# An encoder layer with long convolutions: weight loads issued from ScalarE, and one row copied instead of loaded

## The chip, the cores and the metric

The kernel runs on one core of one Trainium2 chip. Its time is the device time in microseconds (us), given as the median of 3 runs. A core has five engines, each with its own instruction stream: TensorE (PE) does matrix products, VectorE (DVE), ScalarE (ACT) and GpSimd (POOL) do elementwise work, and SyncE (SP) mainly starts transfers (DMAs) between the chip's memory and the on-chip buffer. In the profile, "PEld" is TensorE's loading of stationary operands, and a name with q behind it ("SPq", "ACTq") is that engine's sequencer: the part that waits and starts transfers.

## The reference

One layer of an encoder is computed in fp32 for two inputs with the same weights: group A, 1024 tokens ("prompt"), and group B, 512 tokens ("sample"), both 1024 features wide.

```python
mod = silu(c) @ ada_w + ada_b                       # six vectors: shift, scale, gate, twice
u = rmsnorm(x) * (1 + sc1) + sh1
z = u @ w_in                                        # 1024 -> 2304 (z_hy), 3 x 768 (q, k, v), 2048 (g)
zc = short_conv(z_hy);  x0, x1, v = split(zc)
y_hy = x0 * long_conv(x1 * v, k2, hyena_d)          # by FFT of twice the length
y_at = dilated_attention(q, k, v, rel_bias)         # 3 groups of 4 heads, dilation 1, 4, 16
g_hy, g_at = split(sigmoid(g))
h = x + gt1 * ((g_hy * (y_hy @ w_hy_br) + g_at * (y_at @ w_at_br)) @ w_out)
y = h + gt2 * (relu(rmsnorm(h) * (1 + sc2) + sh2) @ w_up)**2 @ w_down
```

The filter `k2` of the long convolution is itself computed, by a small network with sines, and is used through its spectrum. In a real FFT the values at frequency zero and at the highest frequency are real, and the kernel keeps the second in the place of the first one's imaginary part. That packed row is the row that the change is about.

## The kernel before, in words

**Layout.** Features lie on the 128 partitions and tokens along the free axis. Group A's tokens take two products of 512 columns, group B's take one.

**Products.** Every large product is done in three passes: each operand is split into a high part and the remainder, and `mm3` (its products are line 750) adds wh·xh, wh·xl and wl·xh over eight blocks of 128 features.

**Units.** The weights come as units, one 128 x 1024 tile (512 KB) for each block of 128 outputs. For each unit:
- `wdma` (line 456) loads the raw tile into a buffer `wr`; there are two of them. Four units have a second chunk, of `w_at`, in a buffer of the common pool.
- `wsplit` makes the two parts: ACT copies the tile to `wh` (line 389, CAST in the profile), and VectorE, or GpSimd in the stage qkvB, subtracts to get `wl` (line 390). When the subtraction has ended the raw buffer is free.
- the unit's body runs the 24 (group B) or 48 (group A) products and evacuates the result.

**The stream.** `stream` (line 471) walks through all units. At unit i it writes into the program, in this order: the load of unit i+2, the split of unit i+1, and the body of unit i. Between the products of the body, `pump` lets side work run: generators for the attention, the filter, the convolutions and the norms, paced by a clock that the program keeps from estimated costs. `finish` completes a side job that a later unit needs.

**Order.** ACT's instructions stand in the order in which the program writes them (it is fixed by hand for the whole kernel). The order on SP, VectorE, GpSimd and TensorE is chosen by a planner that keeps the dependences, but for the start, where TensorE's and VectorE's is fixed too. Nearly all transfers are started by SP: `dma` is SyncE's.

**Stages.** In the order of time: the start; the projections of group A (qkvA and zhyA); its gates (gateA); the projections of group B (qkvB, zhyB) and its gates (gateB); the merge of A and of B (mixA, mixB); the MLPs (ffA, ffB). The convolutions of A run as side work beside group A's projections and gates, those of B beside zhyB, gateB and what follows.

**The convolution** (`conv_gen`) runs three times for each group, once for each third of the 768 channels. `stage1` transforms blocks and stores them to the chip's memory. `middle` (line 934) loads them back in another order (line 894), loads the filter's spectrum in two tiles `ka` (line 939) and `kb` (line 940), each in halves of 64 partitions, and constant matrices (line 882), multiplies by a matrix (line 952), by the spectrum (lines 953 to 956), by a second matrix (line 963), and stores (line 969). Then the tiles are loaded in the last order (line 977), multiplied (line 989), and gated by `x0` (line 993). Up to several `middle` run at once.

In the first `middle` of each convolution the packed row needs care:

```python
if eg == 0:
    dma(ka[64:65, 0], S.spec[th][64:65, 0])
    V.memset(kb[0:1, 0], 0.0)
    V.memset(kb[64:65, 0], 0.0)
```

Row 64 of `ka` has been loaded from row 0 of the spectrum (the upper half of `ka` is a second copy of rows 0 to 63), and line 942 loads row 64 of the spectrum over it: 256 numbers. It can start when the load of that half of `ka` has landed. Row 64 of the spectrum is also what the load of `kb` has put in row 0 of `kb`, which line 943 then sets to zero.

Of the kernel before, what the change touches and what calls it, by code (L numbers as in the profile page):

```python
# [325 lines left out]
def _program(ctx, tc, d, outs):  # L326
# [9 lines left out]
    V, A, T, G_ = nc.vector, nc.scalar, nc.tensor, nc.gpsimd  # L336
    dma = nc.sync.dma_start
# [14 lines left out]
    def nm(s):  # L352
        cnt[0] += 1
        return f"{phase[0]}__{s}{cnt[0]}"

    def g(shape=(1024,), dt=F32):
        return gp.tile([128, *shape], dt, tag="g", name=nm("g"))
# [7 lines left out]
    def pss2():  # L365
        return pss().rearrange("p (a b) -> p a b", a=2)
# [6 lines left out]
    def copy(out, in_):  # L373
        rr[0] += 1
        if rr[0] % CPM:
            A.copy(out, in_)
        else:
            V.tensor_copy(out, in_)
# [70 lines left out]
            yield r[0], 0.0  # L449
        yield 0.0, max(end - clock[0], 0.0)  # L450

    def wdma(u):
        u.raw = []
        for i, (src, n) in enumerate(u.chunks):
            raw = g() if i else wp.tile([128, 1024], F32, tag="wraw", name=nm("wr"))
            dma(raw[:, :n], src)
            u.raw.append(raw)

    def wsplit(u):
# [11 lines left out]
    def stream(units, first=0):  # L471
        n = len(units)
        for i, (name, u) in enumerate(units):
            if i < first:
                continue
            phase[0] = name
            if u.before:
                u.before()
            if i + 2 < n:
                wdma(units[i + 2][1])  # L480
            if i + 1 < n:
                wsplit(units[i + 1][1])
            for c in u.body(u.w):
                pump(c, u.ratio)
            u.w = None
            if u.after:
                u.after()
# [22 lines left out]
    def spread_load():  # L510
        t = g((640,))
        dma(t, d["c_spread"])
        V.tensor_copy(spread, t[:, 0:512].rearrange("p (a b) -> p a b", a=4))
        return t[:, 512:640]
# [52 lines left out]
    def ada_load(qt):  # L567
        wts = []
        for k2 in range(4):
            wt = g((2, 512))  # L570
            w = dma(wt, d["ada1"][qt, k2].rearrange("p (a b) -> p a b", a=2))
            wts.append(wt)
        return wts, w.ins
# [306 lines left out]
    def cmat(src, eg):  # L880
        cm = wp.tile([128, 4, 128], F32, tag="cm", name=nm("cm"), bufs=4)
        dma(cm, src[eg])
        return cm

    def stage2_load(S, s1, eg):

        Q, nt = S.Q, S.nt
        nl = 64 // Q
        v = s1.rearrange("j p c -> (j p) c").rearrange("(q r l e) c -> r l q e c", q=Q, r=2, l=nl, e=nt)
        t = g((4, 256))  # L890
        for r in range(2):
            for l in range(nl):
                p0 = 64 * r + Q * l
                dma(t[p0:p0 + Q], v[r, l][:, 4 * eg:4 * eg + 4])
        return t


    def conv_gen(S, th):
# [35 lines left out]
        def middle(eg):  # L934
            sin = stage2_load(S, s1, eg)
            ka, kb = g((4, 256)), g((4, 256))
            es = slice(4 * eg, 4 * eg + 4)
            for hf in range(2):
                dma(ka[64 * hf:64 * hf + 64], S.spec[th][0:64, es])
                dma(kb[64 * hf:64 * hf + 64], S.spec[th][64:128, es])  # L940
            if eg == 0:
                dma(ka[64:65, 0], S.spec[th][64:65, 0])
                V.memset(kb[0:1, 0], 0.0)
                V.memset(kb[64:65, 0], 0.0)
            cm, cb_ = cmat(S.fw, eg), cmat(S.bw, eg)
            yield 0.0, LLD
            y, vv = g((4, 256)), g((4, 256))
            for ep in range(2):
                e2 = slice(2 * ep, 2 * ep + 2)
                ps = pss2()  # L950
                for ee in range(2):
                    T.matmul(ps[:, ee], cm[:, 2 * ep + ee], sin[:, 2 * ep + ee], start=True, stop=True)  # L952
                V.tensor_tensor(y[:, e2], ps, ka[:, e2], ALU.mult)
                V.scalar_tensor_tensor(vv[0:64, e2], ps[64:128], -1.0, kb[0:64, e2], ALU.mult, ALU.mult)
                V.tensor_tensor(vv[64:128, e2], ps[0:64], kb[64:128, e2], ALU.mult)
                G_.tensor_tensor(y[:, e2], y[:, e2], vv[:, e2], ALU.add)
                yield 0.9, LY if ep else 0.0
            del sin, ka, kb, vv
            so = g((4, 256))
            for ep in range(2):  # L960
                ps = pss2()
                for ee in range(2):
                    T.matmul(ps[:, ee], cb_[:, 2 * ep + ee], y[:, 2 * ep + ee], start=True, stop=True)
                copy(so[:, 2 * ep:2 * ep + 2], ps)
                yield 0.9, 0.0
            for r in range(2):
                for l in range(nl):
                    p0 = 64 * r + Q * l
                    dma(v2[r, l][:, 4 * eg:4 * eg + 4], so[p0:p0 + Q])

        yield from par([middle(eg) for eg in range(nt // 4)], WMID)
        yield 0.0, 3.0
        bt = []
# [661 lines left out]
    u0, u1 = units[0][1], units[1][1]  # L1635
    loads = [ada_load(0)]
    f1u = spread_load()
    wdma(u0)
    loads.append(ada_load(1))
    wdma(u1)  # L1640
    loads += [ada_load(2), ada_load(3)]
    last = loads[3][1]

# [39 lines left out]
def build(arrays):  # L1683
    nc = bacc.Bacc("TRN2", target_bir_lowering=False, num_devices=1)
    d = {n: nc.dram_tensor(n, a.shape, mybir.dt.from_np(a.dtype), kind="ExternalInput").ap()
         for n, a in arrays.items()}
    outs = [nc.dram_tensor(n, s, F32, kind="ExternalOutput").ap()
            for n, s in (("out_a", (8, 128, LA)), ("out_b", (8, 128, LB)))]
    with tile.TileContext(nc) as tc:
        with ExitStack() as ctx:  # L1690
            ctx.enter_context(tc.manual_schedule(engines={mybir.EngineType.Activation}))
            _program(ctx, tc, d, outs)
    return nc
# [10 lines left out]
```

## Time and profile before

| | |
|---|---|
| median of 3 runs | 2721.21 us (2716.90 to 2723.11) |
| the profiled execution | 2719.46 us |
| its span in the trace | 2717.7 us |
| granted clock of TensorE, mean | 0.976 of full speed |
| busy: PE / PEld / DVE / ACT / POOL | 2622.7 / 2123.4 / 1217.9 / 861.2 / 241.4 us |
| moved by transfers | 350.97 MB, 129 GB/s over the span |

The span goes from the first to the last event in the trace of one execution; the 1.8 us between it and that execution's own time lie around it. "Busy" counts the time in which an engine works on an instruction; waits, and the starting of transfers, are not counted. Engines work side by side, so their busy times do not add up to the span. A row of the timeline gives the start and the length in us, the engine, the line, the operation, output <- inputs, and in brackets how long the engine had waited before it and for whom. A row of the waits gives who waited at which line, for whom, and then the total in us, the number of waits and the longest.

### The profile page before, as it was taken

The numbers are of one execution on the slowest core, as the hardware profiler recorded it, in microseconds if no ns is written. First come the engines' busy times: TensorE is split into PE (matmuls) and PEld (weight loads), VectorE is DVE, ScalarE is ACT, GpSimd is POOL, SyncE is SP. The second block draws the span as 40 slices with busy tenths as digits, with TensorE's granted clock in tenths as the row PEclk, the third lists the DMA queues.
The fourth block names the chain that finished last, engine by engine and source line by source line (L and its number), as shares of the span: only waits on it lengthen the run. The fifth ranks groups of instructions, "written<-read, shape, count | busy, mean of one in ns | idle before, by whom it ended". The sixth has DMA issues, their size and how long they took to land.

```text
span 2717.7 us, 30781 instructions
## 1 busy us (share of the span) xinstructions
PE 2622.7 (97%) x12296; PEld 2123.4 (78%) x12296; DVE 1217.9 (45%) x1566; ACT 861.2 (32%) x1414; POOL 241.4 (9%) x162
## 2 busy tenths in 40 slices
PE   7999799999999999998999999999999999999999
PEld 4778687778788777777787887888888888888887
DVE  4454352443567633464334455333333333554544
ACT  3543312243243354443243243122112211232322
POOL 0101110100001243000012221000000000000000
PEclk8999898999999999999999999999999999999999
DMA  6355576615655432467663343111111111422322
GB/s 255 120 159 168 169 197 178 195 52 148 197 193 205 151 128 99 132 190 212 218 226 105 120 163 113 47 49 45 55 47 48 54 47 47 147 100 94 99 95 101
DMA packets 138113, 350.97 MB, mean 129 GB/s; under 512 B 19023, under 2 KB 50316, under 8 KB 137843
## 3 DMA queue, kind: packets, MB, share of 16 engines
q1 hardware_dynamic: 137682, 348.23, 39.3%
q8 instruction: 97, 1.59, 0.2%
q0 software_dynamic: 288, 0.79, 0.1%
q14 instruction: 46, 0.37, 0.0%
HBM read 280.68 MB, written 71.16 MB: 129 GB/s over the span
## 4 chain that ended last, share of the span: by engine, by line
PE 56%; DVE 2%; DMA 2%; ACT 1%; issue 1%; SPq 1%; POOL 0%; DVEq 0%; ACTq 0%; POOLq 0%
PE ffA__mm L750 26%; PE ffB__mm L750 13%; PE mixA__mm L750 6%; PE qkvB__mm L750 2%; PE gateB__mm L750 2%; PE zhyB__mm L750 2%; PE mixB__mm L750 2%; DMA convB__g<-convB__dr 1%; PE convB__s L989 1%; ACT attB__sc L1221 0%; DMA convB__g<-filtB__dr 0%; PE convB__s L952 0%; PE filtB__s L872 0%; DVE mixB__wl L390 0%; PE attB__s L1231 0%
## 5 line engine op out<-in xcount | busy, mean ns | idle before, releaser
L750 PE MATMUL ffA__mm<-ffA__g,ffA__wh 128*128 128x512 f32 x1024 | 274.1, 389 | 0.0
L750 PE MATMUL ffA__mm<-normA__g,ffA__wh 128*128 128x512 f32 x992 | 265.2, 389 | 0.0
L750 PEld LDWEIGHTS ffA__mm<-ffA__g,ffA__wh 128*128 128x128 f32 x1024 | 192.0, 188 | 40.5 <-issue 0.4
L750 PEld LDWEIGHTS ffA__mm<-normA__g,ffA__wh 128*128 128x128 f32 x992 | 186.2, 188 | 38.6
L1486 DVE SCALAR_TENSOR_TENSOR mixA__g<-ffA__mm,adam,mixA__g 128x1024 f32<-128x1024 f32 x64 | 82.1, 1283 | 190.1 <-PE ffA__mm L750 190.1
L750 PE MATMUL ffB__mm<-ffB__g,ffB__wh 128*128 128x512 f32 x512 | 157.7, 389 | 0.0
L750 PE MATMUL ffA__mm<-ffA__g,ffA__wl 128*128 128x512 f32 x512 | 157.7, 389 | 0.0
L750 PE MATMUL zhyA__mm<-init__g,zhyA__wh 128*128 128x512 f32 x512 | 150.3, 412 | 7.2 <-DVE zhyA__g L1012 5.6
L750 PE MATMUL ffA__mm<-normA__g,ffA__wl 128*128 128x512 f32 x496 | 152.8, 389 | 0.0
L750 PE MATMUL ffB__mm<-normB__g,ffB__wh 128*128 128x512 f32 x496 | 152.7, 389 | 0.0
L389 ACT CAST ffA__wh<-ffA__wr 128x1024 fp32r<-128x1024 f32 x63 | 66.0, 1048 | 256.7 <-PE ffA__mm L750 213.7
L1468 DVE SCALAR_TENSOR_TENSOR ffA__g<-ffA__mm,ffA__g 128x1024 f32<-128x1024 f32 x32 | 39.2, 1225 | 222.8 <-ACT ffA__g L1467 222.8
L750 PE MATMUL gateA__mm<-init__g,gateA__wh 128*128 128x512 f32 x480 | 132.4, 396 | 0.0
L750 PE MATMUL qkvA__mm<-init__g,qkvA__wh 128*128 128x512 f32 x416 | 120.5, 407 | 0.0
L750 PE MATMUL mixA__mm<-mixA__g,mixA__wh 128*128 128x512 f32 x424 | 116.0, 395 | 3.8 <-DVE mixA__g L390 3.3
L750 PEld LDWEIGHTS zhyA__mm<-init__g,zhyA__wh 128*128 128x128 f32 x512 | 95.5, 192 | 30.2 <-ACT zhyA__wh L389 7.9
L750 PEld LDWEIGHTS ffB__mm<-ffB__g,ffB__wh 128*128 128x128 f32 x512 | 96.0, 188 | 20.3 <-ACT ffB__g L389 0.2
L750 PEld LDWEIGHTS ffA__mm<-ffA__g,ffA__wl 128*128 128x128 f32 x512 | 96.1, 188 | 20.0
L1467 ACT ACTIVATE ffA__g<-ffA__mm 128x1024 f32<-128x1024 f32 x32 | 33.0, 1030 | 237.9 <-PE ffA__mm L750 237.9
L750 PEld LDWEIGHTS ffB__mm<-normB__g,ffB__wh 128*128 128x128 f32 x496 | 93.1, 188 | 19.3
L750 PEld LDWEIGHTS ffA__mm<-normA__g,ffA__wl 128*128 128x128 f32 x496 | 93.1, 188 | 19.3
L750 PEld LDWEIGHTS gateA__mm<-init__g,gateA__wh 128*128 128x128 f32 x480 | 90.4, 190 | 19.0 <-issue 0.6
(487 smaller groups left out, 5105.2 us busy)
## 6 DMA issues: line engine op xcount, KB each, us to landing
ada__g<-ada SPq DMA_DIRECT2D x32, 512.0 KB
ffA__wr<-w_up SPq DMA_DIRECT2D x32, 512.0 KB
ffA__wr<-w_dn SPq DMA_DIRECT2D x32, 512.0 KB
ffB__wr<-w_dn SPq DMA_DIRECT2D x32, 512.0 KB
ffB__wr<-w_up SPq DMA_DIRECT2D x30, 512.0 KB
filtA__dr<-filtA__g SPq DMA_DIRECT2D x24, 512.0 KB
convA__g<-filtA__dr SPq DMA_DIRECT2D x48, 256.0 KB
init__g<-ada SPq DMA_DIRECT2D x16, 512.0 KB
```

The source lines that it names most:

```text
L389: A.copy(hi, raw)
L750: T.matmul(ps[:, 512 * c:512 * c + 512], ww[:, sl], xx(k)[:, 512 * c:512 * c + 512], start=k == 0 and p == 0, stop=k == kt - 1 and p == 2)
L989: T.matmul(ps[:, :, 4 * j8:4 * j8 + 4], bt[j // 4][:, j % 4, 128 * cc:128 * cc + 128], ibm, start=True, stop=True)
L1467: A.activation(r, ps[:, :L], AF.Relu)
L1468: V.scalar_tensor_tensor(r, ps[:, :L], 0.0, r, ALU.max, ALU.mult)
L1486: V.scalar_tensor_tensor(S.h(m), ps[:, :L], mod(S, 5, m), S.h(m), ALU.mult, ALU.add)
```

## The change

The weight loads of `wdma` are started from ACT's queue (`A.dma_start`) and no longer from SP's. The first two units, which are loaded ahead of the stream, are still loaded from SP. All other transfers stay where they were. As ACT's order is that of the program, the load of unit i+2 stands on ACT right ahead of the cast of unit i+1 (or behind side work that was written before it).

The one-row load of line 942 is replaced by a copy on VectorE from row 0 of `kb`, ahead of the memset that sets that row to zero. It happens six times: once in each convolution of each group. `V` is VectorE and `A` is ScalarE.

```diff
-    def wdma(u):
+
+    def wdma(u, issue=A.dma_start):
         u.raw = []
         for i, (src, n) in enumerate(u.chunks):
             raw = g() if i else wp.tile([128, 1024], F32, tag="wraw", name=nm("wr"))
-            dma(raw[:, :n], src)
+            issue(raw[:, :n], src)
             u.raw.append(raw)
...
             if eg == 0:
-                dma(ka[64:65, 0], S.spec[th][64:65, 0])
+                V.tensor_copy(ka[64:65, 0], kb[0:1, 0])
                 V.memset(kb[0:1, 0], 0.0)
                 V.memset(kb[64:65, 0], 0.0)
...
-    wdma(u0)
+    wdma(u0, dma)
     loads.append(ada_load(1))
-    wdma(u1)
+    wdma(u1, dma)
```

## The prediction

> **What bounds the kernel now.** I read the page first, then the table of engine time in stretches of 50 us, then the waits, then the timelines around each stall of TensorE (PE).
>
> ```profile
> span 2717.7 us, 30781 instructions
> PE 2622.7 (97%) x12296; PEld 2123.4 (78%) x12296; DVE 1217.9 (45%) x1566; ACT 861.2 (32%) x1414; POOL 241.4 (9%) x162
> PEclk8999898999999999999999999999999999999999
> PE 56%; DVE 2%; DMA 2%; ACT 1%; issue 1%; SPq 1%; POOL 0%; DVEq 0%; ACTq 0%; POOLq 0%
> ```
>
> PE is busy for 2622.7 of 2717.7 us, so at most 95 us are idle. A change in who issues loads removes no product. It can only change those idle microseconds, and the stretches in which PE ran at a lower granted clock. In the next rows the columns are the stretch, its length, busy time of PE, PEld, DVE, ACT and POOL (with instruction counts), granted clock, DMA share and GB/s.
>
> ```profile
> 400.00:450.00 50.00, 46.19 (x222) 40.21 (x221) 15.45 (x23) 15.53 (x24) 2.58 (x2) 0.83 0.77 224
> 1200.00:1250.00 50.00, 42.07 (x198) 34.89 (x197) 24.36 (x33) 14.69 (x22) 5.17 (x4) 0.90 0.74 221
> 1250.00:1300.00 50.00, 44.30 (x203) 35.61 (x201) 24.25 (x32) 16.76 (x25) 5.18 (x4) 0.99 0.71 204
> 1300.00:1350.00 50.00, 47.88 (x221) 39.98 (x222) 17.40 (x21) 10.85 (x15) 6.14 (x4) 0.94 0.71 229
> 2450.00:2500.00 50.00, 50.00 (x222) 41.43 (x221) 24.22 (x28) 13.95 (x17) 0.00 (x0) 1.00 0.29 101
> ```
>
> The MLP (the last row stands for it) keeps PE full at full clock with DMA at 29%. The idle time lies in the long convolutions' stretches, where DMA is 71 to 77% busy and the clock falls. So the question is what the change does there, and whether it breaks the MLP.
>
> **The change, part 1: loads leave SP.** 266 loads (264 main weight tiles less the two first, and four `w_at` tiles) leave SP's queue for ACT's. Each costs its queue 0.33 us:
>
> ```profile
> L456 SPq DMA_DIRECT2D ffB__wr<-w_dn x32: 327/328/328, 2380.3 to 2695.8; - x32
> SPq L456 <- DVE ffA__wl L390: 624.6, 63, 13.8
> SPq L942 <- DMA convA__g<-filtA__dr: 15.2, 3, 5.6
> SPq L942 <- DMA convB__g<-filtB__dr: 12.0, 3, 4.3
> SPq L571 <- DMA init__g<-xa: 5.1, 5, 1.4
> ```
>
> 266 x 0.328 = 87 us more on ACT, which goes from 861 to about 948 us, 35% of the span. By itself that binds nothing. SP's 624.6 us of waiting for VectorE's subtraction (line 390) in group A's MLP is a load waiting for its raw buffer, with nothing urgent behind it. On ACT that wait would hold compute. Line 456 for unit i+2 now stands on ACT right ahead of the cast (389) of unit i+1, and needs the subtraction of unit i. That subtraction precedes unit i's products, and the cast behind the load waits for the products of unit i-1 anyway. So this wait is nearly always over: 0. Were DVE late, the evacuations, exponentials and casts behind the load on ACT would wait with it.
>
> **Part 2: how late the loads get, the MLP.** Until now a load went out as soon as its buffer was free, about two units ahead of its cast. Now it goes out one cast ahead. The tightest place is group B's MLP:
>
> ```profile
> 2606.40 1.05 ACT L389 CAST ffB__wh<-ffB__wr 128x1024 fp32r<-128x1024 f32 x1
> 2611.84 1.05 ACT L389 CAST ffB__wh<-ffB__wr 128x1024 fp32r<-128x1024 f32 x1
> 2615.22 1.05 ACT L389 CAST ffB__wh<-ffB__wr 128x1024 fp32r<-128x1024 f32 x1 [2.33 <-PE ffB__mm L750]
> ```
>
> Casts stand 5.44 us apart, once per group 3.38 us. A 512 KB load on a quiet queue takes about 3.6 us from issue to the cast that waits for it (1294.58 to 1298.18, rows below). So in the tight place the cast comes 0.33 + 3.6 - 3.38 = 0.55 us late. Its products start a unit (5.44 us) after it, less 1.05 for the cast and 1.2 for the subtraction: 3.2 us are spare. Cost 0. Without that cover it would be 0.55 us at 7 such places, 4 us. Group A's units last twice as long: 0.
>
> **Part 3: group B's gates.** Here a weight load is what PE waits for (SP, then ACT, then PE):
>
> ```profile
> 1294.26 0.23 SPq L942 DMA_DIRECT2D convB__g<-filtB__dr  x1
> 1294.58 0.35 SPq L456 DMA_DIRECT2D gateB__wr<-w_g  x1
> 1294.98 0.98 SPq L977 DMA_DIRECT2D convB__g<-convB__dr  x2
> ```
>
> ```profile
> 1284.74 1.05 ACT L389 CAST gateB__wh<-gateB__wr 128x1024 fp32r<-128x1024 f32 x1
> 1298.18 1.04 ACT L389 CAST gateB__wh<-gateB__wr 128x1024 fp32r<-128x1024 f32 x1 [7.95 <-DMA gateB__wr<-w_g]
> ```
>
> ```profile
> 1299.28 0.67 PE L750 MATMUL gateB__mm<-normB__g,gateB__wh 128*128 128x512 f32 x1 [4.24 <-ACT gateB__wh L389]
> 1300.33 3.64 PE L989 MATMUL convB__s<-csq,convB__g 128*128 128x64 f32 x16 [0.38 <-DMA convB__g<-convB__dr]
> 1347.27 1.89 PE L989 MATMUL convB__s<-csq,convB__g 128*128 128x64 f32 x16
> ```
>
> Line 942, the one-row load, waits until the tile that it overwrites has landed, and holds SP. The weight load behind it goes out at 1294.58, ACT casts at 1298.18, PE stands for 4.24 us. After that stall 16 products of line 989 take 3.64 us, and 1.89 us elsewhere: half clock. With the change the load goes out before the cast at 1284.74 and the weights are there by 1293. The stall then has a next limit: line 989 also waits (0.38) for loads issued behind 942 at 1294.98. Those move up too, by up to 4 us (a wait of 942 is 12.0/3 = 4.0 us), but share the engines with one or two more weight loads, 2.3 us each at 229 GB/s. Bounds: -4.24 - 0.38 - 3.0 (6% of clock over 50 us) = -7.6, and 0 if line 989's loads come no sooner. I take -3, the stall less about one load.
>
> **Part 4: loads pushed into bursts.** Elsewhere "one cast ahead" puts a load into a convolution's burst, ahead of which it used to be.
>
> ```profile
> 1235.03 7.08 DMA convB__g<-convB__dr
> 1323.10 7.46 DMA gateB__wr<-w_g
> ```
>
> ```profile
> 1242.24 3.65 PE L989 MATMUL convB__s<-csq,convB__g 128*128 128x64 f32 x16 [6.62 <-DMA convB__g<-convB__dr]
> 431.30 1.08 PE L989 MATMUL convA__s<-csq,convA__g 128*128 128x64 f32 x8 [3.07 <-ACT qkvA__wh L389]
> ```
>
> ```profile
> 1228.80 1.05 ACT L389 CAST zhyB__wh<-zhyB__wr 128x1024 fp32r<-128x1024 f32 x1
> 1231.08 1.04 ACT L389 CAST zhyB__wh<-zhyB__wr 128x1024 fp32r<-128x1024 f32 x1
> 424.30 1.10 ACT L389 CAST qkvA__wh<-qkvA__wr 128x1024 fp32r<-128x1024 f32 x1
> 430.24 1.04 ACT L389 CAST qkvA__wh<-qkvA__wr 128x1024 fp32r<-128x1024 f32 x1
> ```
>
> The transfer that PE awaits at 1242.24 took 7.08 us in a burst. New loads go out just before 1228.80 and 1231.08, so about one (0.52 MB at 221 GB/s = 2.4 us) lands ahead of it. Bounds: -1 (SP issues sooner) and +4.8 (both loads); I take +1.5. At 431.30 likewise, loads before 424.30 and 430.24: bounds 0 and +2.3, taken +1.
>
> **Part 5: 0.33 us on ACT where PE waits for a split.** The waits (total, times, longest):
>
> ```profile
> PE qkvB__mm L750 <- POOL qkvB__wl L390: 3.4, 2, 2.1
> PE mixB__mm L750 <- DVE mixB__wl L390: 3.0, 4, 1.0
> PE zhyB__mm L750 <- DVE zhyB__wl L390: 2.5, 2, 2.2
> PE mixB__mm L750 <- ACT mixB__wh L389: 1.6, 2, 0.8
> ```
>
> Ten waits whose chain runs through the cast, each now 0.33 us later: bounds 0 and +3.3, taken +2.
>
> **Part 6: the copy.** Six one-row loads become six VectorE copies of one partition by 256 numbers. The nearest row is the memset of that shape beside it:
>
> ```profile
> L943 DVE MEMSET convB__g<- x3: 272/272/272, 1194.3 to 1292.8; 1x256 f32 x3
> ```
>
> 6 x 0.27 = 1.6 us on an engine that is 45% busy: hidden, or +1.6 uncovered. The copy waits for both tiles' halves, which the two memsets and the multiplication behind them wait for already. What goes is 15.2 + 12.0 = 27 us of SP's waiting; of that part 3 holds what reached PE. For the rest I take -1, bounds -3 and +1.6.
>
> **Sum.** -3 + 1.5 + 1 + 2 - 1 = +0.5 us. The profiled execution took 2719.46 us (2717.7 of span and 1.8 around it), 0.06% under the median 2721.21. So 2719.5 + 0.5 = 2720 us.
>
> The Trainium skill (DMA: Bandwidth & Descriptors, section "Issuing engines are not separate DMA queues") speaks against the change: starting DMAs from several engines "will only save the time on the sequencer it takes to initiate the DMA". By it the gains of parts 3 and 6 fall away and the sum is +4.5, 2724 us. The rows of part 3 differ from it so far: what the load lost at 1294.58 was SP's wait in line 942, not time to initiate.
>
> **The rivals.** *A: the side loads gain most.* With SP free of 456 and 942, the loads of the convolutions go out sooner and three stalls go (4.24, 6.62, 3.07 = 13.9 us), with their low clock (17%, 10% and 6% of 50 us = 16.5 us). Two thirds of the 30 us make 2699 us. For it: SP was held at 942 just ahead of line 977. Against it: the 6.62 and 3.07 are awaited transfers in bursts at 221 to 224 GB/s, where an earlier issue queues.
>
> *B: slower, weights in the bursts.* In each of the six convolution passes (three per group) one weight load comes ahead of the transfer that PE needs next: 2.3 us of stall and 1.75 us (3.64 - 1.89) of half clock after it, 24 us in all, less 4.6 for the stall that goes: 2739 us. It decides once a cast's load falls within about 7 us before such a transfer's landing. For it: parts 4's casts do. Against it: in three of the passes PE has other products to run. The Trainium skill (same page, section "Queues, rings and completion order") says that each DMA engine takes turns between queues; by that a weight load would no longer queue behind a burst but take half of its rate. No run before this one has a second queue, so no row shows it.
>
> *C: it doesn't part the queues.* SP's loads already wait for unrelated earlier ones (line 571 waits for `xa`, which it doesn't touch). If ACT's loads are chained to SP's in this way, they wait for the same transfers, the gain of part 3 is gone and the sum is +3.5: 2723 us.
>
> **How the numbers follow.** Forecast 0.40 (its own range 2711 to 2729), A 0.28, B 0.24, C 0.08. About 0.2% (5.4 us) is what a measurement of this kernel can tell from no change: under 2715.8 is faster, over 2726.6 slower. Faster: A and 0.05 of the forecast's, 0.33. Slower: B, and 0.04 of the forecast's and C's together, 0.28. Same: 0.39. The range runs from a little past A (2699) to a little past B (2739): 2695 to 2742.
>
> **What would show it.** Part 1: a second hardware queue with 266 loads, ACT's waits at line 456 for line 390 near 0. Part 2: 2450 to 2500 still 50.00 busy at clock 1.00. Part 3: no 4.24 us stall before a product of `gateB__mm`, ACT's 7.95 gone. Part 4: line 989's waits in `convB` and `convA` against 6.62 and 3.07. Part 5: the four wait rows grown by a third of a us each time. Rival C would show as ACT waiting at line 456 for a transfer. The forecast is wrong if PE's order changes so that its idle time in 50 to 1665 us moves by over 10 us.

## The result, and the profile after

The changed kernel takes 2759.14 us (median; 2754.24 to 2763.19) against 2720.3 us: a ratio of 1.0143, 95% interval 1.0121 to 1.0164. It is 39 us slower; the prediction had 2720 and its range ended at 2742. The page of the profile of the changed kernel:

```profile
span 2752.5 us, 30554 instructions
PE 2636.4 (96%) x12296; PEld 2132.0 (77%) x12296; DVE 1222.4 (44%) x1572; ACT 862.7 (31%) x1414; POOL 241.8 (9%) x162
q1 hardware_dynamic: 99366, 210.84, 24.4%
q10 hardware_dynamic: 38304, 137.38, 15.2%
```

There are two large queues of transfers now, q1 (SP) and q10 (ACT, with the weights' 137 MB). The span grew by 34.8 us. TensorE is busy 13.7 us longer for the same 12296 products, which goes with a lower granted clock (0.971 of full speed on the mean, 0.976 before), and idle 21.1 us longer.

All lines behind 452 have moved by one (989 is now 990). The stretches of 50 us, columns as before:

```profile
400.00:450.00 50.00, 43.67 (x215) 37.65 (x214) 14.57 (x18) 17.33 (x26) 2.56 (x2) 0.87 0.79 218
1200.00:1250.00 50.00, 41.36 (x182) 32.67 (x180) 25.11 (x35) 14.60 (x21) 5.11 (x4) 0.97 0.64 170
1250.00:1300.00 50.00, 40.38 (x161) 33.48 (x162) 22.59 (x30) 9.79 (x12) 3.70 (x3) 0.83 0.71 198
1300.00:1350.00 50.00, 42.97 (x172) 35.20 (x171) 14.89 (x21) 12.52 (x20) 4.05 (x4) 0.80 0.61 179
2450.00:2500.00 50.00, 50.00 (x222) 41.39 (x222) 23.06 (x26) 14.05 (x19) 0.00 (x0) 1.00 0.25 85
```

The MLP is as full as it was. In group B's convolutions (the second to fourth row) TensorE is idler, and less is moved: 170 to 198 GB/s where it was 204 to 229. Its clock is lower in two of the three stretches (0.83 and 0.80 where it was 0.99 and 0.94) and higher in the first (0.97 where it was 0.90). As the kernel runs late there, equal times do not hold quite the same work; the next table goes by the work.

**Where it is lost.** ACT's casts of the 264 weight tiles (line 389) come in the same order in every kernel, so the same cast can be compared. The table gives how much later than in the kernel before it comes, counted from the first cast, each column from one profiled execution. The columns behind the first are experiments that follow. Two executions of kernels that take the same time can differ by 9 us here: copy_only, an experiment below with the median of before, was profiled in its slowest execution and stands at +8.9 at the 98th cast.

| cast (its time before) | changed | pool_pinned | sp_tied_pinned | after_pinned | three_and_bt |
|---|---|---|---|---|---|
| the 37th, A's projections end (691 us) | +10.4 | +4.7 | +0.2 | +10.9 | +0.6 |
| the 77th, B's convolutions begin (1112 us) | +6.7 | +9.3 | +0.1 | +10.1 | +0.4 |
| the 98th, B's convolutions nearly done (1339 us) | +36.3 | +31.2 | +10.9 | +38.2 | -6.2 |
| the last, MLP of B (2702 us) | +36.0 | +30.1 | +16.7 | +36.5 | -6.3 |

In the changed kernel some 7 us come with group A's convolutions and 30 with group B's. From there on to the end nothing is added. From the 77th to the 98th cast the same 42.4 MB are moved, in 256.5 us where it was 226.9, at a granted clock of 0.874 where it was 0.925; TensorE is busy 15.7 us longer there and idle 13.9 us longer.

**What is late there.** The transfers on the chain of waits (start, duration), between 1160 and 1400 us, in the kernel before:

```profile
1204.28 4.37 DMA convB__g<-convB__dr
1208.67 3.99 DMA convB__g<-filtB__dr
1235.03 7.08 DMA convB__g<-convB__dr
...
1288.67 5.53 DMA convB__g<-filtB__dr
1294.98 5.21 DMA convB__g<-convB__dr
```

and after:

```profile
1199.09 7.52 DMA convB__g<-filtB__dr
1222.05 9.33 DMA convB__g<-filtB__dr
1247.10 2.52 DMA convB__dr<-convB__g
1249.70 3.97 DMA zhyB__wr<-w_z
1253.66 9.73 DMA convB__g<-convB__dr
...
1319.04 10.47 DMA convB__g<-convB__dr
```

From issue to landing, the spectrum's loads on these rows (`filtB`) took 5.3 us (the chain leaves the first after 3.99) and 5.5, and now take 7.5 and 9.3; the loads of line 978 (977 before, `convB__dr`, 512 KB, at 1235.03 and 1294.98) took 7.1 and 5.2 and now take 9.7 and 10.5. The two do not have the same cause, as the experiments show; the account of part 4, under "Why the prediction was wrong", comes back to it.

### The profile page after: what moved, and what is told of

The parts are those of the page before. It is cut to its first block, busy times and chain, and to the rows that moved or that the text cites. A ratio compares the mean times of both kernels' runs of the same rounds, so it can differ in the third digit from the quotient of the medians.

```text
span 2752.5 us, 30554 instructions
## 1 busy us (share of the span) xinstructions
PE 2636.4 (96%) x12296; PEld 2132.0 (77%) x12296; DVE 1222.4 (44%) x1572; ACT 862.7 (31%) x1414; POOL 241.8 (9%) x162
## 4 chain that ended last, share of the span: by engine, by line
PE 57%; DMA 3%; DVE 2%; ACT 1%; issue 1%; SPq 1%; POOL 0%; DVEq 0%; ACTq 0%; POOLq 0%
PE ffA__mm L751 25%; PE ffB__mm L751 13%; PE mixA__mm L751 6%; PE gateB__mm L751 3%; PE qkvB__mm L751 2%; PE mixB__mm L751 2%; PE zhyB__mm L751 2%; DMA convB__g<-convB__dr 1%; DMA convB__g<-filtB__dr 1%; PE convB__s L990 1%; PE convB__s L953 0%; DMA convB__dr<-convB__g 0%; ACT attB__sc L1222 0%; PE filtB__s L873 0%; DVE normA__g L711 0%
## 5 line engine op out<-in xcount | busy, mean ns | idle before, releaser
L751 PEld LDWEIGHTS ffA__mm<-normA__g,ffA__wl 128*128 128x128 f32 x496 | 93.1, 188 | 19.3
```

Of the source, the lines that this page charges most:

```text
L751: T.matmul(ps[:, 512 * c:512 * c + 512], ww[:, sl], xx(k)[:, 512 * c:512 * c + 512], start=k == 0 and p == 0, stop=k == kt - 1 and p == 2)
```

## The experiments

"Before" was run beside each group, at 2719.3 to 2720.9 us. The five theories, numbered as in the expectations: 1, ScalarE stands behind its own loads, which wait for SP's; 2, the second queue itself; 3, the copy; 4, the late issue; 5, the planner's other order.

| run | median, us | ratio to before, 95% interval |
|---|---|---|
| copy_only | 2721.09 | 1.0004 [0.9992, 1.0016] |
| act_only | 2756.08 | 1.0129 [1.0104, 1.0154] |
| load_behind_cast | 2755.04 | 1.0122 [1.0099, 1.0144] |
| pool_queue | 2737.19 | 1.0059 [1.0040, 1.0079] |
| act_1k | 2764.33 | 1.0161 [1.0146, 1.0176] |
| pool_1k | 2743.92 | 1.0086 [1.0071, 1.0101] |
| sp_tied | 2733.01 | 1.0040 [1.0026, 1.0054] |
| raw_three | 2718.82 | 0.9999 [0.9989, 1.0008] |
| pool_tied | 2743.92 | 1.0079 [1.0064, 1.0094] |
| bt_late_before | 2719.03 | 0.9993 [0.9984, 1.0003] |
| bt_late_after | 2746.56 | 1.0090 [1.0075, 1.0105] |
| after_pinned | 2754.24 | 1.0122 [1.0105, 1.0139] |
| pool_pinned | 2745.00 | 1.0093 [1.0078, 1.0108] |
| pool_tied_pinned | 2751.86 | 1.0112 [1.0097, 1.0127] |
| sp_tied_pinned | 2734.59 | 1.0050 [1.0035, 1.0065] |
| act_three_pinned | 2758.61 | 1.0144 [1.0124, 1.0164] |
| three_and_bt | 2713.16 | 0.9977 [0.9966, 0.9988] |

### The two parts of the change

copy_only is the kernel before with this alone; act_only is the changed kernel with this taken back.

```diff
-                dma(ka[64:65, 0], S.spec[th][64:65, 0])
+                V.tensor_copy(ka[64:65, 0], kb[0:1, 0])
```

> The copy on VectorE alone; the weight loads stay on SP. Theory 1 (chain): ScalarE loses the time because each weight load that it starts first waits for an earlier, unrelated transfer of SP. Theory 2 (traffic): with a second queue the convolutions' loads take longer to land (977: 5.7 us before, 10.8 us after). Theory 3 (copy): VectorE's copy waits for both spectrum tiles and holds VectorE. By 1 and 2 this kernel is no slower than before, 2713 to 2721 us, as SP's 27 us of waits in line 942 go. By 3 it is slower by most of the loss, 2740 us or more.

> The weight loads on ScalarE alone; the one-row load stays on SP. Theories 1 and 2: all of the loss is here, 2755 to 2770 us. Theory 3: within 5 us of before, 2715 to 2726 us.

The copy is worth nothing, and the loads on ACT make the loss: theory 3 falls. In copy_only, whose slowest execution is the profiled one, the gain that the prediction had put on line 942 can be followed, in the timeline of SP, ACT and PE:

```profile
1293.36 0.38 SPq L456 DMA_DIRECT2D gateB__wr<-w_g  x1
...
1302.02 1.04 ACT L389 CAST gateB__wh<-gateB__wr 128x1024 fp32r<-128x1024 f32 x1 [9.06 <-DMA gateB__wr<-w_g]
...
1303.12 0.79 PE L750 MATMUL gateB__mm<-normB__g,gateB__wh 128*128 128x512 f32 x1 [5.34 <-ACT gateB__wh L389]
```

In the kernel before this load goes out at 1294.58, and this execution runs 2.7 us behind it here (the spectrum's last load: 1292.04 against 1289.31). So the load goes out 3.9 us sooner, and its cast comes 8.66 us after it instead of 3.60. SP waited in line 942 until the spectrum had landed; without that wait the weights wait in the queue, behind the same spectrum, as far as this one place shows.

### ScalarE standing behind its own loads

load_behind_cast is the changed kernel with two steps of `stream` exchanged.

```diff
-            if i + 2 < n:
-                wdma(units[i + 2][1])
             if i + 1 < n:
                 wsplit(units[i + 1][1])
+            if i + 2 < n:
+                wdma(units[i + 2][1])
```

> As the changed kernel, but the load of unit i+2 stands behind the cast of unit i+1 on ScalarE, not ahead of it. A wait of the load then no longer holds that cast; the load goes out about 1 us later. Theory 1: the part of the loss that runs through late casts goes, 2725 to 2745 us. Theory 2: the same loads share the same stretches, 2753 to 2765 us.

pool_queue is the changed kernel with GpSimd in ScalarE's place.

```diff
-    def wdma(u, issue=A.dma_start):
+    def wdma(u, issue=G_.dma_start):
```

> As the changed kernel, but the weight loads are started from GpSimd's queue, whose transfers are counted on semaphores of their own. No load waits for a transfer of SP, and no cast stands behind a load. The convolutions' loads still meet a second queue. Theory 1: most of the loss goes, 2712 to 2735 us. Theory 2: the loss stays, 2745 to 2765 us, and the loads of line 978 take about 10 us as they do after.

The changed kernel does have ACT standing in front of loads. From its timeline and its waits:

```profile
1315.55 0.34 ACTq L457 DMA_DIRECT2D gateB__wr<-w_g  x1
1315.92 1.04 ACT L389 CAST gateB__wh<-gateB__wr 128x1024 fp32r<-128x1024 f32 x1 [5.61 <-DMA convB__dr<-convB__g]
```

```profile
ACT qkvA__wh L389 <- DMA convA__g<-filtA__dr: 14.8, 1, 14.8
ACT gateB__wh L389 <- DMA convB__dr<-convB__g: 7.5, 2, 5.6
ACT gateB__wh L389 <- DMA convB__g<-filtB__dr: 6.8, 1, 6.8
ACT zhyB__wh L389 <- DMA convB__dr<-convB__g: 4.7, 2, 3.2
ACT qkvA__wh L389 <- DMA convA__dr<-convA__g: 1.4, 1, 1.4
```

Seven waits, 35 us, for transfers of SP that neither the load nor the cast touches: the transfers of both queues are counted on the same eight semaphores in turn, and a transfer goes out when the earlier one on its semaphore has landed. It is rival C, and it looked like the cause. But load_behind_cast takes the wait away from the casts (it then stands in front of evacuations, 14 us in five waits) and is no faster beyond the intervals. And pool_queue, without any such wait, keeps 17 us, with line 978's loads at 9.8 us (mean of 4) and the spectrum's at 7.7 (mean of 24 in B's convolutions, 5.4 before); its time lies between what the two theories had said.

### The second queue by itself

In transfers_alone the layer is left out, and patterns of loads are run in its place. In these two, `S` stands for the four loads of 256 KB on SP and "w" for a weight tile, on SP behind them or from ScalarE:

```diff
+        run("w_last", [S, (sp, "w", {})], 0, 3, r)
+        run("w_act", [(act, "w", {}), S], 0, 3, r)
```

> The layer is left out; only transfers are made, six times each, one pattern after the other, each after the last has landed: four loads of 256 KB on SP (as lines 940 and 941) or one of 512 KB in 1 KB pieces (as line 978), alone, with one weight load of 512 KB ahead of them or behind them on SP, or with one started at the same time from ScalarE (4 KB or 1 KB pieces) or from GpSimd. Theory 2 in its simplest form (a second queue takes the order away): behind them on SP the weight load costs the others under 0.5 us, from another queue it costs them 1.5 to 2.5 us, nearly what it costs ahead of them on SP. If the queues don't matter, the other queue costs as little as behind. Theory 2a: 1 KB pieces cost them less than 4 KB pieces do.

The view of the transfers gives the issuing queue, count, size and the median from issue to landing:

```profile
s_alone__x<-w_up SPq DMA_DIRECT2D x24, 256.0 KB, 4.3
w_first__x<-w_up SPq DMA_DIRECT2D x24, 256.0 KB, 5.6
w_last__x<-w_up SPq DMA_DIRECT2D x24, 256.0 KB, 4.4
w_act__x<-w_up SPq DMA_DIRECT2D x24, 256.0 KB, 5.8
w_act1k__x<-w_up SPq DMA_DIRECT2D x24, 256.0 KB, 6.4
w_pool__x<-w_up SPq DMA_DIRECT2D x24, 256.0 KB, 6.4
...
c_alone__x<-w_dn SPq DMA_DIRECT2D x6, 512.0 KB, 3.5
c_wlast__x<-w_dn SPq DMA_DIRECT2D x6, 512.0 KB, 3.6
...
c_wact__x<-w_dn SPq DMA_DIRECT2D x6, 512.0 KB, 5.1
```

A weight load behind the others on their own queue costs them 0.1 us. From ACT's queue it costs them 1.5 us (4.3 to 5.8; line 978's pattern 1.6, from 3.5 to 5.1), as much as ahead of them (5.6). So in these patterns the order on one queue is a priority, and the second queue gives it up. Part of the difference is the time of issue: by the timeline ACT's load goes out at the same moment as the first of the four, and SP's last one 2.4 us after it. In line 978's pattern the two are only 0.4 us apart, and the cost is the same. GpSimd's load goes out some 0.4 us after the first of the four: that one lands as if alone (3.4 to 3.8 us), and the other three bear the delay. Sharing was the guess of theory 2; its lower bound of 1.5 us was met just so.

The Trainium skill (DMA: Bandwidth & Descriptors, section "Queues, rings and completion order") has an engine go round between queues; these rows agree that the queues share.

act_1k is the changed kernel, and pool_1k is pool_queue, with pieces of at most 1 KB asked for.

```diff
-            issue(raw[:, :n], src)
+            issue(raw[:, :n], src, **({} if issue is dma else {'max_dma_last_dim': 1024}))
```

> As the changed kernel, but each weight load is made of pieces of 1 KB, not 4 KB; the order of the instructions is the same on every engine. Theory 2a: the transfer engines take turns between the two queues piece by piece, so the weights' queue now takes less of each turn: lines 940 and 941 land in 6 us or less (7.5 and 8.0 after), and the time falls to 2730 to 2748 us. Theory 2b: it is the bytes in the stretch, or theory 1: ScalarE's waits; then 2752 to 2768 us and no shorter landing of 940.

> As the kernel with the loads on GpSimd's queue, in pieces of 1 KB. Theory 2a: its remaining loss (17 us) shrinks to under 10 us, 2722 to 2731 us. Theory 2b: 2734 to 2745 us.

Only act_1k tries what it was meant to: its trace has 134144 packets of 1 KB on ACT's queue, while that of pool_1k still has packets of 4 KB on GpSimd's (33536 of them, none of 1 KB), so pool_1k says nothing about pieces. Act_1k is no faster than the changed kernel (5 us slower by the medians, with intervals that overlap), and its loads of lines 940 and 941 land no sooner (mean of 12 each in B's convolutions, from the trace's records of issue and landing: 7.7 and 8.3 us, against 7.5 and 8.0). In transfers_alone small pieces cost the others more (6.4 against 5.8). Theory 2a falls: on ACT's queue the share does not shrink with the piece. Pool_1k is 7 us slower than pool_queue with each engine's instructions in the same order; why is not known.

### Late issue, and one unit sooner

sp_tied is copy_only, and pool_tied is pool_queue, with this in `wdma`:

```diff
+        prev = next((i for i in reversed(ins) if i.engine == mybir.EngineType.Activation), None)
...
+            tc.add_manual_dep(x.ins, prev.name, mybir.DependencyInfo(
+                mybir.DependencyClass.Sync, mybir.DependencyReason.DATA), reason="tie")
```

> One queue again: the weight loads are started by SP, but each is made to wait until the ScalarE instruction written ahead of it is done, so that it goes out about as late as in the changed kernel. Theory 4 (late issue alone costs): 2740 to 2760 us. Theories 1 and 2 (the second queue, the shared counts): within 8 us of before, 2715 to 2728 us.

> As the kernel with the loads on GpSimd's queue (2737 us), but each load is made to wait until the ScalarE instruction written ahead of it is done: second queue and late issue together, without ScalarE standing behind a load. If late issue and the second queue make the whole loss, 2750 to 2760 us. If ScalarE's own standing (theory 1) is a large part, 2735 to 2747 us.

raw_three is copy_only with a third buffer, and one buffer less in the common pool.

```diff
-            raw = g() if i else wp.tile([128, 1024], F32, tag="wraw", name=nm("wr"))
+            raw = g() if i else wp.tile([128, 1024], F32, tag="wraw", name=nm("wr"), bufs=3)
...
-            if i + 2 < n:
-                wdma(units[i + 2][1])
+            if i + 3 < n:
+                wdma(units[i + 3][1])
```

> The copy, the loads on SP, a third raw buffer (one buffer of the common pool less), each load one unit sooner. If the stall of group B's gates (4.24 us, ScalarE waiting up to 9 us for a load behind a burst) is a matter of when the load goes out, it goes: 2708 to 2717 us. If the order of the queue sets it, no change: 2717 to 2724 us.

Late issue on one queue costs 14 us by the medians (11 by the ratio), between the two theories' figures; SP then also waits for ACT, with the convolutions' loads behind it, so this may be more than lateness alone. pool_tied, at 2744 us, spoke for theory 1: 15 us were missing to the changed kernel. Raw_three removes the stall of the gates (no wait for `gateB__wh` above 1 us is left on TensorE in B's convolutions) and gains nothing: line 989 now waits at that place, for the convolution's own loads (timeline of PE).

```profile
1301.48 3.64 PE L989 MATMUL convB__s<-csq,convB__g 128*128 128x64 f32 x16 [3.31 <-DMA convB__g<-convB__dr]
```

### The products behind the loads

bt_late_before and bt_late_after are the kernel before and the changed kernel with another number behind the loads of line 977 (978).

```diff
-        yield 0.0, 4.0
+        yield 0.0, 10.0
```

> The kernel before with one number changed: the wait that the program assumes between the loads of line 977 and the products of line 989 is 10 instead of 4, so that more other products are placed between them. If the stalls at line 989 (6.62, 3.07, 1.83, 1.05 us and the low clock behind them) are a matter of place, they go: 2700 to 2714 us. If the work only waits elsewhere: 2715 to 2728 us.

> The same number changed in the changed kernel. If its loss runs through TensorE standing at line 990 for loads that land 4 to 5 us later, it gains more than the kernel before does: 2730 to 2748 us. If the loss runs through ScalarE, it stays: 2750 to 2762 us.

The same number gains 2 us before, within the noise, and 12.6 us after. So a third of the loss depends on where TensorE's products stand around these loads: its waits at line 990 for them fall from 19.3 us (10.1 and 9.2, shown below) to 7.9. The number also moves other products, and the waits for loads at line 953 grow from 7.2 to 19.1 us in this one execution; so by which waits the 12.6 us go is not shown.

### TensorE held in the order of before

In the kernels so far the planner also orders TensorE anew: by the names in the traces, 841 of the 12296 places hold another product in the changed kernel than before. Four kernels hold it in the order of the kernel before, and so differ in the queue and the time of issue, and in what the planner does on VectorE, GpSimd and SP.

```diff
+        for x, y in zip(perm, perm[1:]):
+            tc.add_manual_dep(mine[y], mine[x].name, mybir.DependencyInfo(
+                mybir.DependencyClass.NoSync, mybir.DependencyReason.DATA), reason="pin")
```

> The changed kernel, with TensorE's instructions held in the order that they have in the kernel before (the planner had moved some 200 of them, and here moves none). Theory 5 (the planner's other order makes the loss): 2735 us or less. Theories 1, 2 and 4 (the second queue, the shared counts, the late issue): 2750 to 2766 us.

> The kernel with the loads on GpSimd's queue, TensorE in the order of before. Theory 2 (the second queue itself): 2731 to 2742 us. Theory 5: 2717 to 2726 us.

> The kernel with the loads on GpSimd's queue and tied to ScalarE's order, TensorE in the order of before. Second queue and late issue without ScalarE standing: 2738 to 2750 us; what is missing from there to the changed kernel held in the same order is ScalarE's standing behind loads that wait for SP's transfers.

> One queue, loads tied to ScalarE's order, TensorE in the order of before. If late issue costs by itself: 2728 to 2740 us. If it was the planner's other order: 2717 to 2725 us.

Theory 5 falls: 2754 against 2759 us. pool_tied's 2744 becomes 2752, so what it spoke for was TensorE's order. With the order held, late issue alone costs 14.5 us, the second queue alone (GpSimd's) 25, both 32, and the loads on ACT 34. The 25 are 3 us more than theory 2 had allowed. On the chain of pool_pinned the convolutions' loads are as slow as after the change, though no ACT instruction stands behind a load:

```profile
1198.43 8.17 DMA convB__g<-filtB__dr
...
1250.19 10.24 DMA convB__g<-convB__dr
1283.04 8.28 DMA convB__g<-filtB__dr
...
1314.66 10.01 DMA convB__g<-convB__dr
```

In sp_tied_pinned, with one queue, the spectrum's loads on the chain keep about the time they had (the row of 8.16 us is one of line 978's loads, which are slow here too):

```profile
1211.30 6.08 DMA convB__g<-filtB__dr
1238.23 8.16 DMA convB__g<-convB__dr
...
1272.76 5.68 DMA convB__g<-filtB__dr
```

The last two kernels, the first with TensorE held, combine edits shown above: act_three_pinned is after_pinned with the edit of raw_three, three_and_bt is raw_three with the 10.0 of bt_late_before.

> The changed kernel with TensorE in the order of before (2754 us) and with a third raw buffer, each load written one unit sooner on ScalarE: the second queue and ScalarE's standing stay, the late issue goes. If lateness is its own term on top of the second queue (7 us between the two kernels with GpSimd's queue): 2742 to 2750 us. If the second queue alone makes the loss: 2750 to 2758 us.

> All loads on SP, the copy, a third raw buffer with loads one unit sooner, and 10 instead of 4 for the assumed wait ahead of line 989: each alone took one stall away and gained nothing, as the next one took its place. If the two stalls shield each other, both together gain: 2702 to 2714 us. If the convolutions' chain of transfers sets the end of these stages, nothing: 2715 to 2722 us.

Loads one unit sooner on ACT help nothing (2758.6 against 2754.2 us), though between 1160 and 1400 us they go out 23.3 us ahead of their casts on the mean, against 12.4: on ACT's queue lateness shows no term of its own. On GpSimd's, late issue added 7 us by the medians, with intervals that overlap. The two stalls of the kernel before had shielded each other, as far as two kernels with an order of TensorE of their own can show: without both the kernel takes 2713.2 us, 0.9977 of before (0.9966 to 0.9988), faster than both kernels of this case, with all loads on SP.

## Why the prediction was wrong

**Part 1** held: ACT has the 266 loads, its busy time is unchanged, and its waits for line 390 are few (zhyB 3.2, zhyA 2.1, qkvB 1.4, mixB 0.6 us). What it left out is ACT's wait for other transfers, which stood under rival C.

**Part 2** held: from the fourth unit of A's MLP to the last of B's, 125 casts, the distance to the kernel before changes by under 0.1 us, but for one unit near the end (0.5).

**Part 3 (-3)** failed: not the wait but the burst held the load. With SP's wait gone the load took 8.66 us to its cast instead of 3.60. The prediction's "3.6 us on a quiet queue" and its landing by 1293 took the load out of a burst that it stays behind with or without line 942. In the changed kernel this load does go out right ahead of the cast before it, at 1315.55, but lands 8.1 us later. The stall of `gateB__mm` falls from 4.24 to 1.95 us, and that of line 990 behind it grows from 0.38 to 4.56: 6.5 us together where it was 4.6.

**Part 4 (+1.5 and +1)** is the step that failed most. It gave two transfers one load of delay each, at the two places where a stall stood. The delay falls on many convolution loads that share a stretch with weight loads: over B's convolutions the spectrum's loads of lines 940 and 941 took 2.3 and 2.4 us longer (means of 12 each, from the trace's records of issue and landing: 5.1 to 7.5, 5.6 to 8.0). This goes with the second queue in every kernel of this case: the mean of these 24 loads is 5.4 to 5.9 us in the seven kernels of the layer with all weight loads on SP, and 7.1 to 8.4 in the twelve with a second queue. The loads of line 978 took 5.1 us longer (means of the 4 in B's first two passes: 5.7 to 10.8; the two of the third are unchanged), but this is not the second queue's doing alone: they take 8.8 us in copy_only, which is no slower than before, and 6.5 in act_only, which has the whole loss. Without line 942's wait SP issues them sooner, and they stand in the queue instead. The two stalls named stayed near what they were bounded to, but one that was nearly nothing (0.38 us before line 989 in B's second pass) became as long:

```profile
437.63 2.58 PE L990 MATMUL convA__s<-csq,convA__g 128*128 128x64 f32 x11 [5.13 <-DMA convA__g<-convA__dr]
...
1263.54 6.84 PE L990 MATMUL convB__s<-csq,convB__g 128*128 128x64 f32 x31 [5.57 <-DMA convB__g<-convB__dr]
...
1317.02 0.73 PE L751 MATMUL gateB__mm<-normB__g,gateB__wh 128*128 128x512 f32 x2 [1.95 <-ACT gateB__wh L389]
...
1329.64 3.64 PE L990 MATMUL convB__s<-csq,convB__g 128*128 128x64 f32 x16 [4.56 <-DMA convB__g<-convB__dr]
```

TensorE's waits for the convolutions' loads in all (who waits for whom: total, times, longest), before:

```profile
PE convB__s L989 <- DMA convB__g<-convB__dr: 7.0, 2, 6.6
...
PE convA__s L989 <- DMA convA__g<-convA__dr: 4.4, 6, 1.8
PE convB__s L952 <- DMA convB__g<-convB__dr: 1.3, 2, 0.7
PE convB__s L952 <- DMA convB__g<-filtB__dr: 0.7, 1, 0.7
```

and after:

```profile
PE convB__s L990 <- DMA convB__g<-convB__dr: 10.1, 2, 5.6
PE convA__s L990 <- DMA convA__g<-convA__dr: 9.2, 5, 5.1
...
PE convA__s L953 <- DMA convA__g<-convA__dr: 2.9, 1, 2.9
PE convB__s L953 <- DMA convB__g<-filtB__dr: 2.5, 1, 2.5
PE convB__s L953 <- DMA convB__g<-convB__dr: 1.8, 1, 1.8
```

That is 26.5 us against 13.4, and the low clock behind each comes on top. The upper bounds of part 4 (+4.8, +2.3) were bounds on two stalls, not on the stage: where it took +2.5 for both, some 7 us came with A's convolutions and 30 with B's. How 2.3 us on a load add up to these 30 was not followed step by step. The prediction's last sign of being wrong, another order of TensorE with idle time moved by over 10 us, did show (16.5 us more idle between 50 and 1665 us), but with the order held the loss stays.

**Part 5 (+2)** was about right in size and does not matter: of its four rows qkvB fell to 2.5 us, mixB `wl` and zhyB grew by 1.9 and 2.7, mixB `wh` fell by 1.2; +2.5 in all.

**Part 6 (-1)** held as zero: six copies of 0.285 us, and copy_only within noise.

**Rival A** asked for a gain from SP's freedom; copy_only shows none. **Rival B** had the sign, the mechanism and the place, with 2739 us. Its price was too low: it took one load of 2.3 us and 1.75 us of low clock in each of six passes, where the spectrum's loads are late in all of B's passes, and some 30 us come together there. **Rival C** was right that the queues are not parted, in 35 us of ACT's waits, but wrong in what follows: it thought that only the gain of part 3 would be lost. Its cost by itself looks small, as far as GpSimd's queue can stand for ACT's: with TensorE's order held, loads on ACT take 1.0122 (1.0105 to 1.0139) and loads on GpSimd, tied and without ACT standing, 1.0112 (1.0097 to 1.0127).

The rule of the Trainium skill that spoke against the change (DMA: Bandwidth & Descriptors, section "Issuing engines are not separate DMA queues": nothing is saved but the issue) was right that parts 3 and 6 gain nothing. The sum by it, 2724 us, missed what the runs show: the other queue also takes away an order that the kernel lived by.

**What stays open.** The second queue alone was tried on GpSimd only, whose load cost its neighbours more than ACT's in transfers_alone (6.4 against 5.8 us) and whose waits stand in front of GpSimd's own adds; so the 25 us are not ACT's figure. A kernel with ACT's queue and semaphores apart from SP's was not tried. Late issue on one queue costs 14 us though the spectrum's loads keep their time (5.5 us on the mean); by which path was not followed.

## What to carry to other kernels

Where transfers already keep the DMA engines busy (71 to 77% of the time in these stretches), look at who is ahead of whom before loads are moved to another queue: on one queue a load behind is nearly free for those ahead (0.1 us here), on another it costs as much as one ahead (1.5 us), and the chain with the least slack pays. Judge a load by when it lands, not by how long it took: line 978's loads took longer in copy_only because they went out sooner, and cost nothing. A wait on the issuing queue whose end coincides with the end of a burst may hold nothing, as line 942's did here; the load behind it would wait in the burst. And where removing one stall gains nothing, the next one may stand right behind it: two edits that were each worth nothing gave 7 us together.

## What was not expected of the hardware

- Loads in 1 KB pieces did not leave more to the other queue: its loads took 6.4 us against 5.8 beside 4 KB pieces, and the whole kernel was no faster.
- With the second queue the stage moved less in a given time, not more: from the 77th to the 98th cast 165 GB/s against 187.
